# The gated norm of a state space branch: statistics on 128x512 tiles, or on 128x4 with a diagonal product that spreads them

## The chip, the cores and the metric

The kernel runs on one core of a Trainium2 chip. The metric is the device time of one execution in microseconds, the median of several runs. Besides the runs there is one execution recorded by the hardware profiler; all rows of views come from it.

## The reference

One layer of a hybrid decoder on 512 tokens of 1024 features, in float32. An RMS norm and a wide input projection feed three parallel branches: windowed attention in three groups, causal pooling, and a state space branch (SSD). Each has an output projection (`w_a`, `w_b`, `w_c`) and a sigmoid gate; their gated sum goes through `w_o` to the residual, and a convolutional feed-forward stage and a final norm follow. The change is in the gated norm at the end of the state space branch:

```python
y = ssd_scan(xs, dt, A, Bm, Cm) + d_skip[:, None] * xs
y = y.reshape(b, s, SSD_INNER) * jax.nn.silu(z)
yg = y.reshape(b, s, SSD_GROUPS, SSD_INNER // SSD_GROUPS)   # 2 halves of 512 features
yg = yg * lax.rsqrt(jnp.mean(yg * yg, axis=-1, keepdims=True) + NORM_EPS)
y = yg.reshape(b, s, SSD_INNER) * norm_w
...
merged = gates[:, :, 0] * y_a + gates[:, :, 1] * y_b + gates[:, :, 2] * (y @ w_c)
```

For each token and each half of 512 features there is one factor: the reciprocal root of the mean square.

## The kernel before

Features lie on the 128 partitions and tokens along the row, so a tile of 128x512 holds 128 features of all 512 tokens. A large product is done three times, since each operand is split into a high part and the rest (`wh`, `wl` for weights; `uh`/`ul`, `ah`/`al`, `yth`/`ytl` for activations): `wh` with the high part, `wh` with the low part, `wl` with the high part. For 1024 input features that is three blocks of eight products for one 128x512 result, called a column group below; all of them run on line 234.

The work is a list of jobs, each with up to 1 MB of weights. While a job's products run, its `prepare` splits the next job's weights (`low`, VectorE, line 215), casts those of the one after (`cast`, ScalarE, line 195) and loads a third (`fetch`, SyncE). Two buffers hold raw weights; a load waits until the splitting of the weights two jobs back is done. Side work is written as generators: `step()`, called after each column group (or two), advances every one of them to its next `yield`. `yield WHOLE` lets an item go on last in its step. TensorE, VectorE, ScalarE and GpSimd keep the order in which the code issues; SyncE's DMAs are placed by a scheduler. Row tiles come from a ring of 54 buffers (`T`), and results in PSUM from two pools of four banks (`MM` for column groups, `SM` for side work).

The stretch around the change is given by the string `MIX = "ZZ0zz1ggggaa"`. `Z` and `z` are projection jobs for the two halves' gates `z`, and `g` are the four jobs of the third branch gate, each of two column groups. `a` are the two jobs of the attention output with `w_a`, each of four groups of nine products (three blocks of three). `0` and `1` start the norms `y_norm(0)` and `y_norm(1)`. Behind it comes `w_c`, which multiplies the normed `y` (`YT`).

- `gated` multiplies `y` by `z` (line 1031), squares it on ScalarE (1033), and adds the squares of the four tiles, on GpSimd and last on VectorE (1037).
- `y_norm(gi)` multiplies the 512 summed squares by a matrix of ones (`pss`, line 1046). Every partition then holds the sum of each token, 128x512. Root, reciprocal and one Newton step run on that shape (1048 to 1055). Then each of the four tiles of `y` is scaled (1058), cast (`yth`, 1060) and split (`ytl`, 1065).
- `combine` and `split_o(c)` close the attention: GpSimd weights nine tiles `o` (754) with factors that SyncE spreads from memory (`wb`, 752). VectorE adds three of them to one (760), ScalarE casts it (`ah`, 762), and VectorE splits it (`al`, 765), for c = 0, 1, 2. The `a` jobs multiply these three pairs.
- `rstd_of(ss, cols, n)` exists in the kernel for other norms: mean plus epsilon, root on ScalarE, reciprocal and Newton step on VectorE, all on 128 x `cols`.

Of the kernel before, what the change touches and what calls it, by code (L numbers as in the profile page):

```python
# [10 lines left out]
F32 = mybir.dt.float32  # L11
F32R = mybir.dt.float32r
AF = mybir.ActivationFunctionType
OP = mybir.AluOpType
AX = mybir.AxisListType

P = 128
S = 512
D = 1024
KD = D // P  # L20
EPS = 1e-6
# [62 lines left out]
def trunk(ctx: ExitStack, tc, out, x, rel_bias, ln1_g, w_in, b_gate, w_a, pool_w, pool_scale, w_b,  # L84
# [3 lines left out]
    act, dve, pool, pe, sp = nc.scalar, nc.vector, nc.gpsimd, nc.tensor, nc.sync  # L88
# [5 lines left out]
    cpool = ctx.enter_context(tc.tile_pool(name="const", bufs=1))  # L94
# [13 lines left out]
    def T(name, dt=F32, shape=(P, S)):  # L108
        return big.tile(list(shape), dt, name=name, tag="t")
# [4 lines left out]
    def SM(name):  # L114
        return psum.tile([P, S], F32, name=name, tag="sm")

    def small(name, shape, dt=F32):
        return tiny.tile(list(shape), dt, name=name, tag="tiny")

    eye = cpool.tile([P, P], F32, name="eye")  # L120
    tri = cpool.tile([P, P], F32, name="tri")
    ones = cpool.tile([P, P], F32, name="ones")
# [25 lines left out]
    ROWS, WHOLE = 1, 2  # L148
# [269 lines left out]
    def rstd_of(ss, cols, n):  # L418

        sq, v, r, t, r2 = (small(nme, [P, cols]) for nme in ("sq", "v", "r", "rt", "r2"))  # L420
        dve.tensor_scalar(v, ss, 1.0 / n, EPS, OP.mult, OP.add)
        act.activation(sq, v, AF.Sqrt)
        dve.reciprocal(r, sq)
        if cols == 1:
            dve.scalar_tensor_tensor(t, r, v, r, OP.mult, OP.mult)
        else:
            dve.tensor_mul(t, r, r)
            dve.tensor_mul(t, t, v)
        dve.tensor_scalar(t, t, -0.5, 1.5, OP.mult, OP.add)
        dve.tensor_mul(r2, t, r)  # L430
        return r2
# [77 lines left out]
    bias = []  # L509
# [322 lines left out]
    cst = {}  # L832
# [182 lines left out]
    SQ = {0: [], 1: []}  # L1015
# [23 lines left out]
    def y_norm(gi):  # L1039
        while len(SQ[gi]) < 4:  # L1040
            yield
        yield
        yield
        yield WHOLE
        ps = SM("pss")
        pe.matmul(ps, ones, SQ[gi][0], start=True, stop=True)
        r, t = T("rr"), T("rt")
        act.activation(r, ps, AF.Sqrt, bias=eps, scale=1.0 / S)
        yield
        dve.reciprocal(r, r)  # L1050
        act.activation(t, r, AF.Square)
        yield
        dve.scalar_tensor_tensor(t, ps, S * EPS, t, OP.add, OP.mult)
        dve.tensor_scalar(t, t, -0.5 / S, 1.5, OP.mult, OP.add)
        dve.tensor_tensor(r, r, t, OP.mult)
        for j in range(4):
            y, m = Y[gi][:, j, :], 4 * gi + j
            dve.scalar_tensor_tensor(y, y, cst["dgc"][:, 8 + m:9 + m], r, OP.mult, OP.mult)
            yh, yl = T("yth", F32R), T("ytl", F32R)
            act.copy(yh, y)  # L1060
            YT[m] = (yh, yl)
            if j % 2:
                yield
                for q in (m - 1, m):
                    dve.tensor_sub(YT[q][1], Y[gi][:, q % 4, :], YT[q][0].bitcast(F32))
# [353 lines left out]
    def program():  # L1419
# [26 lines left out]
        for token in MIX:  # L1446
            if token in many:
                yield next(many[token])
            else:
                yield Call(lambda i=int(token): waiting.append(y_norm(i)))  # L1450
# [31 lines left out]
    act.dma_start(g8[:KD, :P], ln1_g[0].rearrange("(k p) -> k p", p=P))  # L1482
    dve.memset(ones, 1.0)
    dve.memset(warm, 1.0)
    eps = cpool.tile([P, 1], F32, name="eps")
    dve.memset(eps, EPS)
    act.activation(warm, warm, AF.Sqrt)
    first = [MM("pa") for _ in range(4)]

# [63 lines left out]
    for tb in range(2):  # L1553
        s0, s1, v, sq, r, rt = (small(n, [P, 1]) for n in ("s0", "s1", "v", "sq", "r", "rt"))
# [26 lines left out]
    r = rstd_of(ss, 2, D)  # L1581
    for tb in (2, 3):
        for h in range(2):
            t = xin[tb, h]
# [97 lines left out]
```

## Time and profile before

| | |
|---|---|
| median of 3 runs | 1050.77 us (1050.66 to 1052.44) |
| profiled execution | 1051.12 us, with a span of 1049.3 us |
| busy share of the span | TensorE 98%, its weight loads 82%, VectorE 62%, ScalarE 45%, GpSimd 15% |
| `pss` of the two halves starts at | 524.85 and 547.48 us |
| the four `g` jobs on TensorE | 525.30 to 570.11 us |
| the two `a` jobs on TensorE | 570.11 to 594.94 us |
| the two reciprocals of 128x512 | 529.45 and 562.01 us, about 3.35 us each |

A timeline row gives the start in us from the beginning of the span, the time to the end of the last of the merged instructions, engine, source line, operation, result and operands, and their count. In brackets stand the idle time ahead of it and what ended that. A row of waits gives the total, the number of times and the longest. A row of a tile gives the shortest, median and longest duration in ns and the first and last start. A fp32 product is recorded as two passes, so four products show as x8. A window row gives its length, busy time and count, granted TensorE clock (1.00 is full speed), share of the DMA engines, and GB/s.

### The profile page before, as it was taken

What the parts mean: (1) busy time and instruction counts of PE and PEld (TensorE: products, weight loads), DVE (VectorE), ACT (ScalarE), POOL (GpSimd) and SP (SyncE); (2) the same over time, 40 slices, a digit from 0 to 9 for tenths busy, and PEclk for the clock granted to TensorE, in tenths of its full rate; (3) what the DMA queues carried; (4) which work ended last, traced back from release to release, by engine and by line L of the source; (5) the groups of instructions that cost most, each with busy time, mean ns of one, the idle gap of its engine ahead of it and who ended that gap; (6) DMA issues with size and microseconds to landing.
All of it is one profiled execution on the core that took longest, in us unless ns stands there. A gap on an engine that the chain in (4) does not pass through costs nothing.

```text
span 1049.3 us, 13068 instructions
## 1 busy us (share of the span) xinstructions
PE 1031.3 (98%) x5198; PEld 864.2 (82%) x5198; DVE 652.1 (62%) x859; ACT 469.0 (45%) x758; POOL 153.1 (15%) x125
## 2 busy tenths in 40 slices
PE   8999999999999999999997999999999999999997
PEld 8988878898888878888886888898888888878885
DVE  4563566684366558766769556766766556556645
ACT  5432554442564364557545224545444443433331
POOL 1680000000000005110171500001111111110110
PEclk9999999999999999999999999999999999999999
DMA  8445312126222444442243426643232322362332
GB/s 260 138 115 147 104 58 74 31 65 196 81 81 81 120 120 117 129 138 81 81 113 100 141 81 220 209 162 115 81 121 81 111 90 84 117 240 65 117 101 81
DMA packets 119788, 121.81 MB, mean 116 GB/s; under 512 B 5523, under 2 KB 101590, under 8 KB 119727
## 3 DMA queue, kind: packets, MB, share of 16 engines
q1 hardware_dynamic: 119135, 120.12, 37.0%
q8 instruction: 41, 0.67, 0.3%
q10 hardware_dynamic: 592, 0.86, 0.2%
q14 instruction: 20, 0.16, 0.0%
HBM read 115.07 MB, written 4.32 MB: 114 GB/s over the span
## 4 chain that ended last, share of the span: by engine, by line
PE 92%; DVE 3%; DMA 2%; issue 1%; ACT 1%; POOL 1%; SPq 0%; ACTq 0%; DVEq 0%; POOLq 0%
PE pa L234 30%; PE pu L234 22%; PE pb L234 17%; PE pqk L234 9%; PE pa L1534 2%; PE p L234 2%; PE ps L662 1%; PE pu L1353 1%; PE ppw L234 1%; PE pt L690 1%; PE po L703 1%; PE py L988 1%; DVE wl L215 1%; DMA raw<-in_w_in_dram 1%; DMA eye<-in_c_eye_dram 1%
## 5 line engine op out<-in xcount | busy, mean ns | idle before, releaser
L215 DVE TENSOR_TENSOR wl<-raw,wh 128x2048 fp32r<-128x2048 f32 (+3 forms) x95 | 217.2, 2288 | 76.1 <-ACT wh L195 38.6
L195 ACT CAST wh<-raw 128x1024 fp32r<-128x1024 f32 (+3 forms) x188 | 189.5, 1026 | 66.5 <-DVE raw L337 21.1
L234 PE MATMUL pa<-uh,wh 128*128 128x512 f32 x384 | 98.3, 398 | 0.0
L1189 DVE SCALAR_TENSOR_TENSOR hc<-pu,fcol,hc 128x510 f32<-128x510 f32 x88 | 65.8, 748 | 51.2 <-ACT hc L1186 49.5
L234 PE MATMUL pa<-ul,wh 128*128 128x512 f32 x384 | 94.9, 389 | 0.0
L234 PE MATMUL pa<-uh,wl 128*128 128x512 f32 x384 | 94.8, 389 | 0.0
L234 PEld LDWEIGHTS pa<-ul,wh 128*128 128x128 f32 x384 | 72.1, 188 | 15.1
L234 PEld LDWEIGHTS pa<-uh,wl 128*128 128x128 f32 x384 | 72.1, 188 | 15.0
L234 PE MATMUL pu<-uh,wh 128*128 128x512 f32 (+1 forms) x352 | 83.7, 380 | 0.0
L234 PE MATMUL pu<-ul,wh 128*128 128x512 f32 (+1 forms) x352 | 83.5, 379 | 0.0
L234 PE MATMUL pu<-uh,wl 128*128 128x512 f32 (+1 forms) x352 | 83.5, 380 | 0.0
L234 PEld LDWEIGHTS pa<-uh,wh 128*128 128x128 f32 x384 | 70.4, 188 | 14.8 <-issue 1.0
L234 PEld LDWEIGHTS pu<-uh,wh 128*128 128x128 f32 x352 | 64.1, 188 | 12.6 <-ACT uh L452 0.2
L234 PEld LDWEIGHTS pu<-ul,wh 128*128 128x128 f32 x352 | 64.2, 188 | 12.5
L234 PEld LDWEIGHTS pu<-uh,wl 128*128 128x128 f32 x352 | 64.2, 188 | 12.4
L1186 ACT ACTIVATE hc<-pu,fcol,fcol 128x512 f32<-128x512 f32 x40 | 31.2, 780 | 75.6 <-PE pu L234 75.4
L1194 POOL TENSOR_TENSOR hc<-hc 128x512 f32<-128x512 f32 x22 | 31.5, 1432 | 223.4 <-DVE hc L1189 169.3
L950 POOL TENSOR_TENSOR xd<-xc,dec 128x512 f32<-128x512 f32 x6 | 6.3, 1058 | 332.8 <-DVE xc L944 314.1
L1074 ACT ACTIVATE sg<-pa,col 128x512 f32<-128x512 f32 x24 | 16.5, 687 | 53.9 <-PE pa L234 47.7
L683 ACT ACTIVATE sb<-sb,both 128x128 f32<-128x128 f32 (+1 forms) x72 | 30.1, 419 | 23.6 <-DVE both L680 13.4
L234 PE MATMUL pqk<-uh,wh 128*128 128x512 f32 x144 | 36.9, 394 | 0.0
L234 PE MATMUL pqk<-ul,wh 128*128 128x512 f32 x144 | 36.3, 389 | 0.0
(358 smaller groups left out, 1776.8 us busy)
## 6 DMA issues: line engine op xcount, KB each, us to landing
raw<-in_w_in_dram SPq DMA_DIRECT2D x25, 1024.0 KB
raw<-in_ffn_w_up_dram SPq DMA_DIRECT2D x22, 1024.0 KB
raw<-in_w_in_dram SPq DMA_DIRECT2D x20, 512.0 KB
raw<-in_ffn_w_down_dram SPq DMA_DIRECT2D x10, 1024.0 KB
raw<-in_w_o_dram SPq DMA_DIRECT2D x8, 1024.0 KB
raw<-in_w_b_dram SPq DMA_DIRECT2D x4, 1024.0 KB
al<-ad SPq DMA_DIRECT2D x16, 256.0 KB
raw<-in_w_c_dram SPq DMA_DIRECT2D x4, 1024.0 KB
```

Of the source, the lines that this page charges most:

```text
L195: act.copy(job.high[:, :, o], job.raw[:, :, o])
L215: (eng or dve).tensor_tensor(l[:, :, o], job.raw[:, :, o], h[:, :, o].bitcast(F32), OP.subtract)
L234: pe.matmul(ps, l, r, start=first and n == 0, stop=last and n == total - 1)
L662: pe.matmul(pss[i][:, o:o + w * P], q[r, n * P:(n + 1) * P], k[r, kb * P:(kb + w) * P], start=True, stop=True)
L683: act.activation(sb[:, off:off + w * P], sb[:, off:off + w * P], AF.Exp, bias=nm[:, n, h:h + 1], accum_out=ls[:, n, h:h + 1])
L690: pe.transpose(pt[:, o:o + P], sb[:, o:o + P], eye)
L703: pe.matmul(po[DH * hh:DH * hh + DH, n * P:(n + 1) * P], V[g, kb + i][:, (2 * cc + hh) * DH:(2 * cc + hh + 1) * DH], probs[2 * cc + hh, mb ...
L1074: act.activation(s, ps, AF.Sigmoid, bias=col[:, o:o + 1])
L1186: act.activation(t, ps, AF.Identity, bias=ff["c1"][:, ff["b"] + m:ff["b"] + m + 1], scale=fw(2, m))
L1189: dve.scalar_tensor_tensor(t[:, sh:], ps[:, :S - sh], fw(k, m), t[:, sh:], OP.mult, OP.add)
L1194: pool.tensor_tensor(a, a, t, OP.mult)
L1534: pe.matmul(first[2 * n + j][:, lo:hi], a[:, k, j * P:(j + 1) * P], b[:, k, lo:hi], start=a is wh and b is uh and k == 0, stop=a is wl and ...
```

## The change

Per half, the one product `ones` x squares of 128x512 becomes four products of one column: each block of 128 tokens of the summed squares is the stationary operand, one column of ones the moving one, and the sums land as 128x4, tokens on partitions. `rstd_of` turns them into factors on 128x4. VectorE multiplies an identity (repeated four times) by the factors into a 128x512 tile `dg` with four diagonals. Three column groups later the matrix of ones multiplies `dg` into `prb`, which again holds every token's factor on every partition, now in PSUM. The scaling of `y` reads it there. The tile `eps` falls away.

```diff
         yield WHOLE
         ps = SM("pss")
-        pe.matmul(ps, ones, SQ[gi][0], start=True, stop=True)
-        r, t = T("rr"), T("rt")
-        act.activation(r, ps, AF.Sqrt, bias=eps, scale=1.0 / S)
-        yield
-        dve.reciprocal(r, r)
-        act.activation(t, r, AF.Square)
-        yield
-        dve.scalar_tensor_tensor(t, ps, S * EPS, t, OP.add, OP.mult)
-        dve.tensor_scalar(t, t, -0.5 / S, 1.5, OP.mult, OP.add)
-        dve.tensor_tensor(r, r, t, OP.mult)
+        for tb in range(4):
+            pe.matmul(ps[:, tb:tb + 1], SQ[gi][0][:, tb * P:(tb + 1) * P], ones[:, :1],
+                      start=True, stop=True)
+        r = rstd_of(ps[:, :4], 4, S)
+        dg = T("dg")
+        dve.tensor_tensor(dg.rearrange("p (b t) -> p b t", b=4), eye.unsqueeze(1).to_broadcast([P, 4, P]),
+                          r.unsqueeze(2).to_broadcast([P, 4, P]), OP.mult)
+        yield
+        yield
+        yield
+        yield WHOLE
+        ps = SM("prb")
+        pe.matmul(ps, ones, dg, start=True, stop=True)
         for j in range(4):
             y, m = Y[gi][:, j, :], 4 * gi + j
-            dve.scalar_tensor_tensor(y, y, cst["dgc"][:, 8 + m:9 + m], r, OP.mult, OP.mult)
+            dve.scalar_tensor_tensor(y, y, cst["dgc"][:, 8 + m:9 + m], ps, OP.mult, OP.mult)
...
-    eps = cpool.tile([P, 1], F32, name="eps")
-    dve.memset(eps, EPS)
```

The function that it now calls, unchanged:

```python
def rstd_of(ss, cols, n):
    sq, v, r, t, r2 = (small(nme, [P, cols]) for nme in ("sq", "v", "r", "rt", "r2"))
    dve.tensor_scalar(v, ss, 1.0 / n, EPS, OP.mult, OP.add)
    act.activation(sq, v, AF.Sqrt)
    dve.reciprocal(r, sq)
    ...
    dve.tensor_mul(t, r, r)
    dve.tensor_mul(t, t, v)
    dve.tensor_scalar(t, t, -0.5, 1.5, OP.mult, OP.add)
    dve.tensor_mul(r2, t, r)
    return r2
```

## The prediction

> **What bounds the kernel now.** I read the page first, then TensorE's own waits, then TensorE's and VectorE's timelines around the change, the granted clock there, and the chain.
>
> ```profile
> span 1049.3 us, 13068 instructions
> PE 92%; DVE 3%; DMA 2%; issue 1%; ACT 1%; POOL 1%; SPq 0%; ACTq 0%; DVEq 0%; POOLq 0%
> ```
>
> TensorE makes up 92% of the chain that ended last. Work on another engine counts only where TensorE waits for it; anything added to TensorE counts in full. So the next view is what TensorE waited for (total, times, longest):
>
> ```profile
> PE pa L234 <- DVE al L765: 3.2, 1, 3.2
> PE pa L234 <- ACT ah L762: 2.5, 1, 2.5
> ...
> PE pb L234 <- DVE wl L215: 0.5, 1, 0.5
> ...
> DVE sq L1037 <- POOL sq L1037: 7.6, 1, 7.6
> ```
>
> The first two are the longest of the run; the third is the only one listed behind the stage in question, and the last is VectorE's, used below. The two long ones sit right behind the changed norm, where the attention output meets `w_a`. TensorE's timeline there (start, us, instructions):
>
> ```profile
> 562.86 1.98 PE L234 MATMUL pa<-uh,wl 128*128 128x512 f32 x8
> ...
> 570.11 0.61 PE L234 MATMUL pa<-ah,wh 128*128 128x512 f32 x2
> 573.25 0.50 PE L234 MATMUL pa<-ah,wh 128*128 128x512 f32 x1 [2.52 <-ACT ah L762]
> 577.40 0.80 PE L234 MATMUL pa<-al,wh 128*128 128x512 f32 x1 [3.17 <-DVE al L765]
> ...
> 582.68 0.85 PE L234 MATMUL pa<-ah,wh 128*128 128x512 f32 x3
> ...
> 594.94 1.98 PE L234 MATMUL pa<-yth,wh 128*128 128x512 f32 x8
> ```
>
> From 582.68 to 594.94 stand 54 products in 12.26 us: 0.227 us each, 1.82 for eight. The `w_a` stage has 72 products, so it needs 72 x 0.227 = 16.35 us. It took 594.94 - 570.11 = 24.83. **8.48 us are lost in this one stage.** That is more than the two waits, because the clock fell (PE busy, clock, DMA share, GB/s):
>
> ```profile
> 574.00:576.00 2.00, 0.22 (x1) 0.83 0.28 43
> 576.00:578.00 2.00, 0.60 (x2) 0.50 1.08 376
> 582.00:584.00 2.00, 2.00 (x10) 0.97 1.01 344
> ```
>
> At half clock the 13 products from 577.40 to 582.68 took 5.28 us where 13 x 0.227 = 2.95 would do: 2.33 of the 8.48.
>
> Who made TensorE wait? VectorE's queue in that stretch:
>
> ```profile
> 549.67 3.47 DVE L1065 TENSOR_TENSOR ytl<-xs,yth 128x512 fp32r<-128x512 f32 x2
> ...
> 559.24 2.28 DVE L215 TENSOR_TENSOR wl<-raw,wh 128x2048 fp32r<-128x2048 f32 x1
> 562.01 3.35 DVE L1050 RECIPROCAL rr<-rr 128x512 f32<-128x512 f32 x1 [0.49 <-ACT rr L1048]
> ...
> 567.22 0.68 DVE L1053 SCALAR_TENSOR_TENSOR rt<-pss,rt 128x512 f32<-128x512 f32 x1
> 567.93 0.43 DVE L1054 TENSOR_SCALAR rt<-rt 128x512 f32<-128x512 f32 x1
> 568.40 0.69 DVE L1055 TENSOR_TENSOR rr<-rr,rt 128x512 f32<-128x512 f32 x1
> ...
> 574.13 1.29 DVE L1065 TENSOR_TENSOR ytl<-xs,yth 128x512 fp32r<-128x512 f32 x2
> 575.33 1.41 DVE L1058 SCALAR_TENSOR_TENSOR xs<-xs,dgc,rr 128x512 f32<-128x512 f32 x2
> 576.65 0.69 DVE L765 TENSOR_TENSOR al<-o,ah 128x512 fp32r<-128x512 f32 x1
> ```
>
> VectorE works almost without a gap. The `al` at 576.65, which releases TensorE at 577.40, stands behind the second half's norm: the reciprocal and what follows. This is the work that the change takes away or moves back.
>
> **What the change costs on TensorE.** Per half of the features it replaces one 128x512 product `pss` by four one-column products, and adds a 128x512 product `prb` of the shape that `pss` had.
>
> ```profile
> 479.54 1.16 PE L995 MATMUL pyo<-xcv,st 128*128 128x128 f32 x8
> 480.45 2.10 PE L234 MATMUL pa<-uh,wh 128*128 128x512 f32 x8
> 482.39 1.98 PE L234 MATMUL pa<-ul,wh 128*128 128x512 f32 x8
> ...
> 524.85 1.02 PE L1046 MATMUL pss<-sq,ones 128*128 128x512 f32 x2
> 525.30 2.39 PE L234 MATMUL pa<-uh,wh 128*128 128x512 f32 x8
> 527.53 1.98 PE L234 MATMUL pa<-ul,wh 128*128 128x512 f32 x8
> L1046 PEld LDWEIGHTS pss<-sq,ones x4: 188/188/188, 524.6 to 547.5; 128*128 128x128 f32 x4
> ```
>
> `pss` and the block of eight behind it took 527.53 - 524.85 = 2.68, so `pss` itself cost 2.68 - 1.82 = 0.86. `prb` has the same shape and takes its place at the same price. What is left is four one-column products, each with a 128x128 fp32 weight load, recorded as two passes. The trace has no one-column product. Nearest are the four `pyo` products of 128 columns with such weights: 482.39 - 479.54 - 1.82 = 1.03. From above, eight loads end to end at 0.188 give 1.50; from below, loads wholly hidden behind the block before give 0. I take 1.03, since its weights are the same and the loads are what a single column leaves over. Two halves: **+2.06 us** (0 to 3.0), all on the path.
>
> **What it does on VectorE and ScalarE.** The instruction order of the built kernel shows where things now stand. Each half has six operations of 128x4, a root of 128x4, and a diagonal of 128x512. The scaling of `y`, with its splitting, comes three column groups later. For the second half both scaling pairs, and both pairs of `ytl`, now stand behind the last `al`.
>
> ```profile
> L422 ACT ACTIVATE sq<-v x1: 203/203/203, 20.6 to 20.6; 128x2 f32<-128x2 f32 x1
> L423 DVE RECIPROCAL r<-sq x1: 165/165/165, 20.8 to 20.8; 128x2 f32<-128x2 f32 x1
> L427 DVE TENSOR_TENSOR rt<-r x1: 160/160/160, 21.0 to 21.0; 128x2 f32<-128x2 f32 x1
> L964 DVE TENSOR_TENSOR al<-al,cbt x16: 672/682/1779, 392.1 to 475.7; 128x512 f32<-128x512 f32 x16
> ```
>
> ```profile
> 559.35 0.62 ACT L762 CAST ah<-o 128x512 fp32r<-128x512 f32 x1 [2.64 <-DVE o L760]
> 559.99 1.28 ACT L1048 ACT_TABLE_LOAD   x1
> 561.28 0.69 ACT L1048 ACTIVATE rr<-pss,eps 128x512 f32<-128x512 f32 x1
> ```
>
> Ahead of the last `al`, VectorE loses 3.35 + 0.68 + 0.43 + 0.69 = 5.15 of wide norm work, one pair of scalings (1.41) and one pair of `ytl` (1.29): 7.85. It gains six small operations at 0.16 (1.0), the diagonal (0.68, from the multiplication with a repeated operand at line 964) and one new wait: the small reciprocal follows at once on a root that stands on ScalarE behind the cast `ah` and a table load. That is 0.62 + 1.28 + 0.20 = 2.1, less the small `v` that runs beside it: 1.9. Two more waits for ScalarE casts (0.6 each) are no longer covered by other work: that of the first `ytl` pair and that of the second `al`. Sum 4.8. The last `al` ends about 577.34 - 7.85 + 4.8 = 574.3.
>
> TensorE reaches the `w_a` stage at 570.11 + 2.06 = 572.2 and needs the last `al` five products later, at 573.3. That alone leaves at most 1 us.
>
> The tighter place is earlier. The weights' low part `wl` of the last gate job ended at 561.52 and is first used at 562.86. It now stands behind the second half's small norm: 1.0 + 0.68 + 1.9 later, and 0.6 for the cast, so 565.7. TensorE arrives there 1.2 later than before (one `prb`, and twice 1.03 - 0.86), at 564.1. That would be 1.65 us of idle TensorE. It delays the `w_a` stage by the same, so the last `al` is then in time: the two don't add. Something may cover it. The `ytl` pair at 549.67 took 3.47 beside GpSimd's products where a pair takes 1.29 alone. Now the scaling pair, which reads PSUM, stands in that place. If it runs at its 1.41, up to 2.2 are won and the wait is nil. I take 0.6, between 0 and 1.65 and nearer to none, because the row of 3.47 is in just that stretch.
>
> First half: its chain lies in the stretch from 525 to 545, where VectorE later waits 7.6 for GpSimd; its `prb` finds its diagonal ready, and I cost it at nothing beyond TensorE's products. Without that cover it would cost the same 1.9. The `eps` memset lies ahead of the first data; nothing waits for it. SyncE's order changes in one place (a rival below). The `w_c` stage needs the second half's `y` only 16.35 us after the `w_a` stage starts, near 589. Its late scalings and casts add up to some 8 us on VectorE behind 574, so they end in time.
>
> **Sum.** -8.48 + 2.06 + 0.6 = -5.8 us. The profiled execution took 1051.12 us around its span of 1049.3 and gives 1045.3. It lies 0.35 above the median of the runs, 1050.77, so the forecast is **1045.0 us**.
>
> [...]
>
> **Rivals.**
>
> *The wait moves and keeps part of the gain* (chance 0.12). `wl` comes at 565.7 or later, TensorE idles 1.65 to 2.5, and the clock halves after it. For it: the idle from 570.7 to 573.25 was just 2.52 and led to half clock. Against: there another 3.17 followed almost at once; here full work follows. Price 1.65 + 2.33 in place of 0.6: 1048.4.
>
> *SyncE's new order starves GpSimd, and the run is slower* (0.07). Four `wb` transfers now go ahead of the 1 MB of gate weights and the rest behind it.
>
> ```profile
> 532.30 6.40 DMA raw<-in_w_in_dram
> 539.61 3.80 POOL L754 TENSOR_TENSOR o<-o,wb 128x512 f32<-128x512 f32 x3 [6.44 <-DMA wb<-wd]
> ```
>
> GpSimd waited 6.44 for `wb`, and its third product stands ahead of the sum of squares on which VectorE waits. If the third product's `wb` lands later by d, the sum, both following `wl` and the small norm shift by d. At d = 3.5 the idle in front of the last `wl` is 4.1, with 2.33 of half clock the gain is gone; at d = 5 the time is 1050.77 - 8.48 + 2.06 + 5.6 + 2.33 = 1052.3. Against: four of the six transfers needed go first, and as many bytes as before stand ahead of the other two.
>
> *The stall at `w_a` is not the norm's* (0.05): `o` itself comes late, the 8.48 stay and TensorE's 2.06 come on top: 1052.8. Against: VectorE has no idle of note ahead of `al`.
>
> *The gain is given back* (0.04) behind the stage, at a transfer that the wait had covered: 1050.8. Against: no wait over 0.5 us is listed for TensorE behind it.
>
> **How the numbers follow.** The forecast case has 0.72. A measurement can tell about 0.2%, 2.1 us, from no change: faster is under 1048.7. The forecast case and most of the first rival lie there: 0.72 + 0.11 = 0.83. Same: 0.01 of the first rival and 0.03 of the last, 0.04. Slower: 0.07 + 0.05 + 0.01 = 0.13. Range: lowest with no wait and one-column products at nearly nothing, 0.35 a half: 1050.77 - 8.48 + 0.7 = 1043.0. Highest: the first rival with the products at 1.50, 1048.4 + 0.94 = 1049.3.
>
> **What would show it.** In the profile after: no wait on `ah` or `al` over 1 us; the `w_a` stage in 16 to 18 us at full clock; four `pss` products and their load within 1.1 us; a wait for `wl` of 0 to 1.7 in front of the last gate job's third block; `prb` without a wait; `w_c` starting near 589. It is wrong if the stage still takes over 20 us, if TensorE waits over 3 us at `pss`, `prb` or that `wl`, or if `w_c` waits for `yth` or `ytl`.

## The result, and the profile after

The changed kernel takes **1043.48 us** (median of 4 runs, 1042.58 to 1044.57); the kernel before, on the same chip, 1050.72. The ratio is 0.993, 95% interval 0.9912 to 0.9947. Its profiled execution took 1044.23 us around a span of 1042.4, against 1051.12 and 1049.3.

What TensorE waited for (total, times, longest), the whole list but its last two rows of 0.2:

```profile
PE uT L1552 <- DVE v L1558: 2.3, 1, 2.3
PE pa L1493 <- DVE relb L515: 1.1, 1, 1.1
PE pcb L919 <- ACT xcv L1007: 1.0, 1, 1.0
PE pb L234 <- DVE wl L215: 0.5, 1, 0.5
```

The two waits on `ah` and `al` are gone, and none has taken their place. TensorE's timeline of the stretch:

```profile
524.53 0.95 PE L1047 MATMUL pss<-ones,sq 128*128 128x1 f32 x8
525.34 2.11 PE L234 MATMUL pa<-uh,wh 128*128 128x512 f32 x8
527.28 1.99 PE L234 MATMUL pa<-ul,wh 128*128 128x512 f32 x8
...
541.81 1.02 PE L1058 MATMUL prb<-dg,ones 128*128 128x512 f32 x2
542.26 2.41 PE L234 MATMUL pa<-uh,wh 128*128 128x512 f32 x8
544.51 1.98 PE L234 MATMUL pa<-ul,wh 128*128 128x512 f32 x8
...
563.60 1.98 PE L234 MATMUL pa<-uh,wl 128*128 128x512 f32 x8
...
571.75 0.84 PE L234 MATMUL pa<-ah,wh 128*128 128x512 f32 x3
...
588.07 1.98 PE L234 MATMUL pa<-yth,wh 128*128 128x512 f32 x8
```

The `w_a` stage now runs from 571.75 to 588.07: 16.32 us where 24.83 stood. The price is seen ahead of it. The four one-column products cost 527.28 - 524.53 - 1.82 = 0.93, the spreading product 544.51 - 541.81 - 1.82 = 0.88. One half thus adds 0.93 + 0.88 - 0.86 = 0.95. From the first `pss` to the start of `w_a` it is 47.22 us against 45.26: 1.96 more.

Why nothing waits is seen in VectorE's timeline:

```profile
542.93 1.76 DVE L1037 TENSOR_TENSOR sq<-sq 128x512 f32<-128x512 f32 x1 [7.14 <-POOL sq L1037]
544.62 3.37 DVE L215 TENSOR_TENSOR wl<-raw,wh 128x2048 fp32r<-128x2048 f32 x1
547.91 1.39 DVE L1061 SCALAR_TENSOR_TENSOR xs<-xs,dgc,prb 128x512 f32<-128x512 f32 x2
549.34 2.20 DVE L1068 TENSOR_TENSOR ytl<-xs,yth 128x512 fp32r<-128x512 f32 x2
551.46 1.39 DVE L1061 SCALAR_TENSOR_TENSOR xs<-xs,dgc,prb 128x512 f32<-128x512 f32 x2
552.78 1.40 DVE L760 TENSOR_TENSOR o<-o,o 128x512 f32<-128x512 f32 x2
554.10 0.15 DVE L421 TENSOR_SCALAR v<-pss 128x4 f32<-128x4 f32 x1
556.45 0.18 DVE L423 RECIPROCAL r<-sq 128x4 f32<-128x4 f32 x1 [2.19 <-ACT sq L422]
...
558.07 2.28 DVE L215 TENSOR_TENSOR wl<-raw,wh 128x2048 fp32r<-128x2048 f32 x1
...
567.91 0.68 DVE L765 TENSOR_TENSOR al<-o,ah 128x512 fp32r<-128x512 f32 x1
```

GpSimd's and ScalarE's rows of the same stretch, used below:

```profile
533.54 3.40 POOL L754 TENSOR_TENSOR o<-o,wb 128x512 f32<-128x512 f32 x2 [2.79 <-DMA wb<-wd]
540.38 1.29 POOL L754 TENSOR_TENSOR o<-o,wb 128x512 f32<-128x512 f32 x1 [3.44 <-DMA wb<-wd]
...
542.85 7.54 POOL L754 TENSOR_TENSOR o<-o,wb 128x512 f32<-128x512 f32 x4
554.03 2.55 POOL L754 TENSOR_TENSOR o<-o,wb 128x512 f32<-128x512 f32 x2 [3.64 <-DMA wb<-wd]
```

```profile
554.91 1.28 ACT L422 ACT_TABLE_LOAD   x1
556.21 0.21 ACT L422 ACTIVATE sq<-v 128x4 f32<-128x4 f32 x1
```

The last `al` ends at 568.6, 8.7 earlier than before and 4 ahead of its use at 572.9. The last gate job's `wl` ends at 560.35, for a use at 563.60.

In the tables below the stretch from the first `pss` to the start of `w_c` is compared between profiles, since the part of the run ahead of it differs by up to 3 us between the profiles (the first `pss` starts between 523.2 and 526.3, and between 524.5 and 525.9 in three profiles of the changed kernel alone). Before it is 594.94 - 524.85 = 70.09; in the changed kernel 63.54. Behind it come 454.4 us before and 454.3 after: nothing is given back.

### The profile page after: what moved, and what is told of

It is laid out like the page before. It is cut to its first block, busy times and chain, and to the rows that moved or that the text cites. A ratio compares the mean times of both kernels' runs of the same rounds, so it can differ in the third digit from the quotient of the medians.

```text
span 1042.4 us, 13096 instructions
## 1 busy us (share of the span) xinstructions
PE 1030.2 (99%) x5214; PEld 864.4 (83%) x5214; DVE 645.8 (62%) x864; ACT 466.9 (45%) x756; POOL 151.1 (14%) x125
## 4 chain that ended last, share of the span: by engine, by line
PE 97%; DVE 1%; ACT 1%; DMA 0%; issue 0%; DVEq 0%; SPq 0%; ACTq 0%
PE pa L234 35%; PE pu L234 22%; PE pb L234 17%; PE pqk L234 9%; PE pa L1535 2%; PE p L234 2%; PE ps L662 1%; PE pu L1356 1%; PE ppw L234 1%; PE pt L690 1%; PE po L703 1%; PE py L988 1%; PE uT L1552 1%; PE pyo L995 1%; PE pst L974 0%; DMA xin<-in_x_dram 0%
```

## The experiments

The theory: VectorE is full in this stretch (before, busy for 9.30 of the 10 us from 560 to 570), TensorE waited for what stood last in its queue, and the change took norm work out from ahead of it; the added products are only a price. Rivals: the small shape is needed wherever the norm stands; the later place alone does it; the first half's chain does it.

| kernel | ratio to before, 95% interval | first `pss` to `w_c` |
|---|---|---|
| wide, second half later (e1) | 0.9964 (0.9949 to 0.9978) | 64.82 |
| narrow, scaling early (e2) | 0.9949 (0.9938 to 0.9961) | 65.23 |
| first half narrow (e3) | 0.9992 (0.9983 to 1.0001) | 68.91 |
| before, with filler products (e4) | 0.9975 (0.9964 to 0.9985) | 67.35 |
| second half narrow (e5) | 0.9957 (0.9944 to 0.9970) | 63.48 |
| changed kernel, beside e5 and e7 (e6) | 0.9949 (0.9937 to 0.9960) | 63.54 |
| wide, only the scaling later (e7) | 0.9950 (0.9937 to 0.9963) | 63.31 |
| second half narrow, root and reciprocal apart (e8) | 0.9932 (0.9918 to 0.9946) | 62.54 |
| changed kernel, beside e8 (e9) | 0.9937 (0.9923 to 0.9951) | 63.55 |

**Wide, but later (e1).**

```diff
         act.activation(r, ps, AF.Sqrt, bias=eps, scale=1.0 / S)
         yield
+        if gi:
+            yield
+            yield
+            yield WHOLE
         dve.reciprocal(r, r)
```

> The kernel before with one thing changed: the second half's wide statistics (reciprocal of 128x512 and all behind it) are issued two column groups later, behind the last al; every operation stays 128x512 and TensorE's order is that of before. Theory A (the gain is that VectorE's norm work left its place ahead of al, and the narrow products are only a price): no wait of TensorE at w_a, the w_a stage in 16.3 us at full clock, no added product, so 1050.7 - 8.5 = 1042.2 us, at or under the changed kernel's 1043.5. Rival B (the narrow shape is the gain, since 5.15 us of wide work delay VectorE wherever they stand): the wait moves to the evacuation of the w_a groups or to w_c, at least 3 us of it, and the time is 1045.5 or more.

Measured: 1046.05 us against 1050.31. TensorE's list has new rows:

```profile
PE pa L234 <- DVE sg L1091: 2.1, 1, 2.1
PE pu L234 <- ACT uh L452: 1.6, 1, 1.6
...
PE pa L234 <- ACT yth L1064: 0.7, 1, 0.7
```

The wait for `al` is gone at no added product, but the rival was right that the wide work is paid elsewhere: the stretch is 64.82 where 70.09 - 8.48 = 61.61 would be left without any loss, so 3.2 us are paid. VectorE's timeline of the same run ends the `w_a` stage thus:

```profile
583.85 3.10 DVE L1069 TENSOR_TENSOR ytl<-xs,yth 128x512 fp32r<-128x512 f32 x2
586.88 2.28 DVE L215 TENSOR_TENSOR wl<-raw,wh 128x2048 fp32r<-128x2048 f32 x1
589.08 2.47 DVE L1091 TENSOR_TENSOR sg<-sg,pa 128x512 f32<-128x512 f32 x4
```

Four evacuations of `w_a` groups come only at 589.08, in one go. `w_c` needs one of their PSUM banks and starts at 589.90, though the last three `w_a` products, begun at 586.99, were issued by about 587.7. The queue was shortened ahead of `al` and became too long behind it. The 0.7, at the seventh `w_a` group, is listed under a cast that no `w_a` product reads; that it is an evacuation too is likely (one ends at about 583.3, the group starts at 583.47), but not shown. The 1.6 at `pu` stands at the start of the feed-forward stage; other kernels have 0 to 0.5 there, and its cause was not followed.

**Narrow, but early (e2).**

```diff
         yield
         yield
-        yield
-        yield WHOLE
         ps = SM("prb")
```

The diff is against the changed kernel, and it moves the scaling of both halves.

> The changed kernel with the spreading product and the scaling issued two column groups behind the four one-column products, where the kernel before has its scaling, in place of three. Ahead of the last al VectorE then has two scaling pairs and one ytl pair more, 1.4 + 1.4 + 1.3 = 4.1 us, less the 0.7 that it waited for the cast ah. The last al ends at 568.6 + 3.4 = 572.0 and is needed at 572.9. Theory A with the shorter queue as its main part: no wait or one under 1 us, 1043.5 to 1044.5 us. Rival (the later place of the scaling is what removed the wait, the small shape counts little): a wait of 3 us or more at w_a with half clock behind it, 1048 to 1050 us.

Measured: 1045.15 us. No wait at `w_a`, so the small shape removes nearly all of that wait without the later place. But a wait came that I had not foreseen, at the spreading product itself:

```profile
560.28 1.10 PE L1056 MATMUL prb<-dg,ones 128*128 128x512 f32 x2 [1.44 <-DVE dg L1051]
```

The second half's diagonal is ready only at 560.1. In the changed kernel the product is asked for one column group later, at 565.42, and the diagonal, ready at 558.15, has lain there for 7 us. This wait also hides a rest of the other. With it the stretch is 65.23 - 63.54 = 1.69 longer than in the changed kernel, and the third `al` product starts at 573.3, where the last `al` ended at 572.45. TensorE 1.69 earlier would have waited some 0.8 there (an estimate from these times), of 5.7 before.

**First half narrow, second half wide (e3).** The code of the changed kernel under `if gi == 0`, that of the kernel before otherwise.

> Only the first half's norm is narrow, the second half's is as in the kernel before. Theory A: the wait at w_a belongs to the second half, so it stays (5 to 6 us of idle TensorE, the w_a stage over 23 us), and the first half's products add 0.95: 1050.7 + 0.95 = 1051.7 us. Rival C (the gain came from the first half: its shorter chain and SyncE's new order started GpSimd's products and everything behind them earlier): most of the wait is gone, 1044 to 1047 us.

Measured: 1049.74 us, no change that the interval can tell from none. The wait for the last `al` stays, that for `ah` goes:

```profile
569.99 1.15 PE L234 MATMUL pa<-ah,wh 128*128 128x512 f32 x3
...
574.78 0.80 PE L234 MATMUL pa<-al,wh 128*128 128x512 f32 x1 [3.18 <-DVE al L765]
```

Behind it three products took 575.38 to 576.66, 1.28 us where 0.68 is the full pace and 1.28 (577.99 to 579.27) was that of the kernel before at a clock of 0.50. So the second half's norm makes most of the loss, as the theory has it. But the first half is not neutral: the stretch is 1.18 shorter in spite of the 0.95 that its products add, so some 2.1 us come from its earlier chain. I had put that at nothing.

**Filler products (e4).** The kernel before, with 20 products ahead of the `w_a` stage:

```diff
+        def filler():
+            ps = SM("fill")
+            for _ in range(20):
+                pe.matmul(ps, uh[:, 0, :P], uh[:, 1, :], start=True, stop=True)
...
+            if at == MIX.index("a"):
+                yield Call(filler)
```

> The kernel before with 20 products of 128x512 that nobody reads, issued right ahead of the w_a stage: 20 x 0.227 = 4.5 us of work in a place where TensorE idles 6. It measures how much of the 8.5 us is the clock. If the half clock behind the wait costs its 2.3 us by itself: the stage still waits for the last al at 577.4, but runs at full clock from there, and the time is 1050.7 - 2.3 = 1048.4 us, with a granted clock near 1.0 between 576 and 582. If the clock is not set by the idle time: half clock as before, and 1050.7 us or up to 4.5 more.

Measured: 1048.03 us, 2.3 under the kernel before, and the stretch is 2.74 shorter, with more work in it. The wait for the last `al` shrinks to 0.95 in TensorE's timeline, and the clock never falls, as the windows below it show (PE busy, PEld, DVE, ACT, POOL, clock, DMA share, GB/s):

```profile
578.22 0.50 PE L234 MATMUL pa<-al,wh 128*128 128x512 f32 x1 [0.95 <-DVE al L765]
```

```profile
576.00:578.00 2.00, 1.27 (x6) 0.73 (x4) 2.00 (x4) 1.03 (x2) 0.00 (x0) 1.00 0.94 275
578.00:580.00 2.00, 1.78 (x8) 1.49 (x9) 1.81 (x4) 1.52 (x3) 0.00 (x0) 1.00 0.72 249
```

The half clock behind the wait is real time by itself, near the size that the pace of the products gave (2.33): the last `al`, put 0.06 ahead of the start of its product as in the kernel before (an estimate), ends 578.16 - 526.18 = 51.98 behind the first `pss`, where it ended 577.34 - 524.85 = 52.49 behind it, and these 0.51 taken off the 2.74 leave 2.23.

**Second half narrow, first half wide (e5).** As e3, with `if gi == 1`.

> Only the second half's norm is narrow, the first half's is as in the kernel before. After the runs so far: the first half's narrow norm costs TensorE 0.95 and the later place and small size of the second half's remove the wait. In the changed kernel the last al ended at 568.6 and was needed at 572.9, and the last gate job's wl at 560.35 against 563.6, so 2 to 3 us of VectorE work may come back ahead of both without a wait. So no wait at w_a, the w_a stage in 16.3 us, and 0.95 less than the changed kernel: about 1042.5 us. Rival (the first half's earlier chain is needed too): a wait of 1 us or more at that wl or at w_a, and the changed kernel's time or more.

Measured: 1044.62 us where the changed kernel beside it had 1044.29. The stretch, 63.48, is not shorter by 0.95. One wait came back, that for the last gate job's `wl`:

```profile
562.23 2.13 PE L234 MATMUL pa<-uh,wl 128*128 128x512 f32 x8 [0.63 <-DVE wl L215]
```

The rival's condition held in part: with the wide first half that `wl` is late. VectorE idles 2.13 us ahead of it, between the small `v` and the small reciprocal. So the two halves do not add up: the first alone makes the stretch 1.18 shorter (e3), the second alone 6.61, both together 6.55. Beside a narrow second half, the narrow first half gains nothing: what its chain wins, its products cost.

**The changed kernel again (e6).**

> The changed kernel once more, for runs on the same chip as the others: 1043.5 us, 0.993 of the kernel before.

Measured: 1044.29 us, 0.9949; the stretch is 63.54 again, to the hundredth.

**Wide, only the scaling later (e7).**

```diff
         dve.tensor_tensor(r, r, t, OP.mult)
+        if gi:
+            yield
+            yield WHOLE
         for j in range(4):
```

> The kernel before with only the second half's scaling (and its casts and splitting) two column groups later; reciprocal and Newton step keep their place ahead of the last al. Of the 7.85 us taken away ahead of it, 2.7 go and 5.15 stay. If VectorE's work ahead of al counts us for us, the last al ends 2.7 earlier, at 574.6, against 571.2 where TensorE could take it: idle of 3.4 in place of 6.1, with or without the 2.3 of half clock: 1046 to 1048 us. If the later place of the scaling alone had done it: 1042.2 us. If only the statistics count: 1050 us.

Measured: 1044.58 us, a better time than I expected of it. TensorE's timeline:

```profile
572.51 0.50 PE L234 MATMUL pa<-ah,wh 128*128 128x512 f32 x1 [0.53 <-ACT ah L762]
572.85 0.62 PE L234 MATMUL pa<-al,wh 128*128 128x512 f32 x2
574.08 0.50 PE L234 MATMUL pa<-al,wh 128*128 128x512 f32 x1 [0.60 <-DVE al L765]
```

My 2.7 was a wrong count. It was the changed kernel's balance, in which a scaling pair of the first half comes into the stretch. This edit leaves the first half alone and moves both scaling pairs and a `ytl` pair behind the last `al`, 1.4 + 1.3 + 1.4 = 4.1. Measured from the second `pss`, the last `al` ends 25.3 us later, against 29.9 before: 4.6 earlier. What is left is two listed waits of 1.1 together, and the clock does not fall (1.00 from 568 to 578). So the later place alone, with every operation still wide and no product added, gives as much as the change: the reciprocal of 3.35 could have stayed.

**Second half narrow, root and reciprocal apart (e8).** e5 with `rstd_of` written out and one column group between its two engines:

```diff
+            dve.tensor_scalar(v, ps[:, :4], 1.0 / S, EPS, OP.mult, OP.add)
+            act.activation(sq, v, AF.Sqrt)
+            yield
+            dve.reciprocal(r0, sq)
```

> Narrow norm for the second half only, with one column group between the root and the small reciprocal, so that VectorE splits the last gate job's weights (wl) while ScalarE casts ah, loads its table and takes the root. VectorE's 2.1 us of idle ahead of that wl go, and with them TensorE's wait of 0.6 that the narrow second half alone had. From the first pss to the start of w_c: 63.48 - 0.63 = 62.85 us, against 63.54 in the changed kernel and 70.09 in the kernel before; 1043.6 us where the changed kernel has 1044.3. If the idle time of VectorE was not what held that wl: 63.5 again.

Measured: 1042.94 us beside the changed kernel's 1043.29; the two intervals overlap, so the runs alone don't show which is faster. The profile does for the stretch: 62.54 against 63.55. VectorE no longer idles for the root:

```profile
558.87 3.31 DVE L215 TENSOR_TENSOR wl<-raw,wh 128x2048 fp32r<-128x2048 f32 x1
562.11 0.16 DVE L1054 RECIPROCAL r<-sq 128x4 f32<-128x4 f32 x1
```

TensorE has no wait in the stretch, and 62.54 is what the sum gives: 70.09 - 8.51 + 0.95 = 62.53.

**The changed kernel beside it (e9).**

> The changed kernel beside it, for the comparison on one chip: 63.54 us from the first pss to w_c, 0.994 of the kernel before.

Measured: 1043.29 us, 63.55.

## Why the prediction was right

- **The 8.48 us of the `w_a` stage** (waits and half clock) were to go whole: 24.83 became 16.32, 8.51. Of this 2.2 to 2.3 are the clock, which e4 shows by itself.
- **The products, +2.06:** measured +1.96. The nearest row, `pyo` with columns of 128, was a little dear: 0.93 where I took 1.03. Four one-column products cost about as much as the one of 512 columns that they replace (0.86), and the spreading product is the net price.
- **The wait for `wl`, +0.6:** it did not come. This is the term that was off, and with it the last `al`, which I put at 574.3 and which ended at 568.6. I had summed VectorE's queue with GpSimd's slowing of it as before. In fact the scaling that reads PSUM ran at 1.39 a pair beside GpSimd, the `ytl` pair in 2.20 in place of 3.47, and the `o` pair in 1.40 in place of 3.50 while GpSimd waited for its next transfer. The sum of squares came earlier too, by 1.44 counted from the first `pss`. Only the first of these was among the prediction's reasons for no wait. The first half's part of the change brings them: e3, with that part alone, has pairs of 1.39, 2.20 and 1.41; in e5, without it, the `ytl` pair takes 3.47 and the `o` pair 2.39, and the wait is there with 0.63, close to the 0.6.
- **The new wait on ScalarE** was sized right: 2.19 measured against 1.9, and the one for the second `ah` 0.69 against 0.6. The table load ended at 556.19 and the root started at 556.21, right behind it.
- **The small operations** of the second half took 0.15 to 0.18 each, as the rows of 0.16 had it.
- **SyncE's order**, the slower rival: it went the other way. GpSimd's first two products start at 533.5, where the first three started at 539.6, the third at 540.4, and the sum behind them is earlier, not later. That it is SyncE's order that did so, and not the first half's chain, was not separated.
- **The first half, at nothing:** the step that was wrong in kind. e3 gives it some 2.1 us, and e5 shows that without it the last `wl` is late by 0.6. This and the +0.6 for `wl` are one error, and that it was small was luck: beside the narrow second half the first half's gain only pays for its own products.
- **The first rival's ground**, that the idle time of 2.52 led to half clock, is not borne out. The windows of the kernel before give 1.00 up to 574 and 0.83 from 574 to 576; a change from 1.00 to 0.50 within that window lies at about 575.3, in the wait of 3.17 that followed. So the clock was still full after the 2.52, and e3, with the wait of 3.18 alone, has that half pace too (1.28 for three products).

The sum of the prediction, -5.8, became 63.54 - 70.09 = -6.55 in the stretch; the rest to the profiles' 6.9 lies ahead of the first `pss`. The medians of the runs fell by 7.24 here, and by 5.07 and 6.81 in the comparisons of e6 and e9, with the changed kernel's stretch at 63.54 to 63.55 each time; how near a median came to the forecast is thus in part chance. The mechanism is shown, with one limit: of the 7.85 us that leave VectorE's queue, the prediction put 5.15 down to the small shape and 2.70 to the later place, and did not ask whether one of them would do. e7 shows that moving the scaling alone, 4.1 us of the queue, does the same, and e1 that moving the statistics as well moves the wait to the end of the stage. The narrow shape shortens VectorE's whole queue (busy for 652.1 us before, 645.8 after); the later place only reorders it.

## What to carry to other kernels

When the bounding engine waits for the last item of another engine's full queue, count that queue up to the item and see which entries nobody needs yet. Moving those back added no product to the bounding engine here (e7); moving more of them made the same queue late for something behind (2.1 us, e1). Making them small cost products (1.96 us here) but shortened the whole queue. And price a stall by the time that its stage needs at full pace, not by its listed wait: here 5.7 us of waits were 8.5 us of time.

## What the runs showed that I had not expected

- Two operations of 128x4 on VectorE, with two operands in SBUF, took 0.97 and 1.21 us beside GpSimd, where the same ones later take 0.17 and 0.16. They end at 529.52 and 530.76, and GpSimd's operations beside them at 529.50 and 530.75. Each thus ended 0.01 to 0.02 us behind a GpSimd operation; what held it is not shown (rows of the changed kernel, GpSimd's first):

```profile
525.46 4.04 POOL L745 TENSOR_TENSOR nmT<-nmT,dtmp 6x512 f32<-6x512 f32 x3 [19.54 <-DVE dtmp L741]
529.47 1.28 POOL L1037 TENSOR_TENSOR sq<-sq 128x512 f32<-128x512 f32 x1
528.55 0.97 DVE L427 TENSOR_TENSOR rt<-r 128x4 f32<-128x4 f32 x1
529.55 1.21 DVE L428 TENSOR_TENSOR rt<-rt,v 128x4 f32<-128x4 f32 x1
```

- The scaling with one operand in PSUM was not slowed beside GpSimd (1.39 for a pair at 547.91), while the splitting with two operands in SBUF was (3.37 at 544.62 against 2.28 at 558.07, with GpSimd idle from 556.58). The two differ in operation too, and in the kernel before the scaling from SBUF ran only while GpSimd was idle (535.66, 553.07, 569.13, 575.33), so that PSUM is the reason is not shown.
- Idle times of TensorE of 0.5 and 0.6 us close together (e7), of 0.95 (e4) and of 2.06 (e1) left the clock at 1.00, and behind the 1.44 in e2 the products kept the full pace (eight in 1.81 from 563.08). In the kernel before, 2.52 left it at 1.00 too, and in the next wait it fell at about 575.3, 1.1 us after that wait began (577.40 - 3.17 = 574.23). Since 2.52 left the clock alone and 1.1 did not, these runs give no length of idle time at which it falls.
